# Half a stage of lead for the sample units of a hybrid decoder step, with the new values' block summed last

## The chip, the cores and the metric

The kernel runs on one core of one Trainium2 chip. The metric is the device time of one execution in microseconds; the runs shown are given by their median, and one further execution was profiled.

## The reference, cut to what matters

One inference step of a small decoder trunk: one Conformer convolution layer with its feed-forward, then one attention layer with its feed-forward. It is computed for a prompt of 512 new positions and for 8 sample sequences of 8 new tokens each, all in float32. The attention has 16 heads of 64 and three dilation groups, each with its own queries, keys and values:

```python
WINDOWS = (128, 512, 2048); DILATIONS = (1, 4, 16)
k, v = shared_kv(x, pos, p['kv_norm'], p['w_kv'], p['k_norm'])   # per group, k normed and rotated
q = queries(x, pos, p['b_norm'][j], p['w_q'][j], p['q_norm'][j])
for g in range(N_GROUPS):
    if kv_bufs is None:                                   # prompt: a band of blocks
        o, l = band_attention(q[:, :, g], *keyside[g], r, WINDOWS[g] // r)
    else:                                                 # samples: rows of a cache, then the new ones
        kall = concat([buf[:, :, 0], k_new]); vall = concat([buf[:, :, 1], v_new])
        o, l = gathered_attention(q[:, :, g], *gathered(kall, vall))
x = x + merge_groups(outs, lses, p['w_o'][j], x.dtype)    # softmax over the groups, then w_o
```

The sample part reads keys and values of three caches (128, 512 and 1024 rows per sequence) and appends the 8 new rows of each sequence.

## The kernel before, in words

The convolution (its products lie in a four by four arrangement of 32-wide fields of TensorE, sixteen in all) and the first feed-forward come first; the change does not touch them. Then comes `attention`, which has two parts.

**Projection stages.** `stage(s)` for s = 0 to 3 projects four heads (256 columns) of the queries, keys and values: nine chunks, for kinds 0 (query), 1 (key), 2 (value) and groups 0 to 2. A chunk (`chunk`) takes its matrix of weights from `w_next`, loads a later one on SP's queue (`wraw`), multiplies the prompt's rows in four blocks (`mm3`, L228 to L230, names `pj<-whi,xh`) and the samples' rows once (L1147, `pj<-whi,xs`), and yields five times. Rotated and normed rows are stored to DRAM (`scr` for the prompt, `scs` for the samples' new keys and values) by entries of `due`, at most five ticks later. `new_keys` copies the samples' new queries and keys into `Qz` and `KN`.

**Prompt part.** `prompt()` then runs the band attention of the prompt for 32 pairs of half-blocks, software pipelined: scores (`sc`, L1283), maximum on VectorE, exponential on ScalarE, transposes (`tpt`, L1373), values (`po`, L1395). Its operands come back from DRAM (`nat`, `v`, L1080, L1260, L1264); statistics of the groups go through DRAM in small transfers (`sx`, `ot`, `scc`, `cb`). It yields 88 times.

**Sample units.** The sample attention is cut into eight units, `sample_unit(u)`: unit u handles heads of stage s = u // 2 for four of the eight sequences. A unit is a list of steps, registered by `at(i, order)` under the number `LEAD + u * PERIOD + i`, with PERIOD 32 and LEAD 12, so successive units overlap:

- i = -12 to 31, the keys: nine loads of key blocks (`kk`, 512 KB each, five buffers; L909, L911, L860), their 72 transposes (L920), and the scores (L945) for groups 1, 2 and 0 at i = 14, 26 and 29; the last takes the new keys as well.
- i = 32 to 67, the values: one exponential (`SS`, L966), transposes of the weights (L979), ten loads of value blocks (`vv`, four buffers, each eight steps ahead of its use; L999 to L1010) with ten groups of products summed in `pv` (L1018), scaling, and a small product into `as` (L1031).

Block ti = 1 of the ten holds the new values; it is loaded from `scs` (L1002, three loads of 32 KB), which the value chunks of the same heads have written.

`weave` merges lists of yields by their numbers: the k-th of n goes in at (k + 1) / n. The first 12 sample steps are merged into the end of stage 0, 64 steps into each of stages 1 to 3, and the remaining 100 into the prompt part:

```python
weave((stage(0), 45), (first_loads(), 45))
weave((stage(s), (45, 45, 45)[s - 1]), (islice(samples, WIN[s - 1]), WIN[s - 1]))
weave((prompt(), 2 * NM + 24), (samples, NSAMPLE - LEAD - sum(WIN)))
```

So unit 0's keys run in the first half of stage 1, its values in the second half together with unit 1's keys, and so on; the prompt part runs the values of units 5, 6 and 7 and the keys of units 6 and 7. Every engine executes in the order in which the merged code stands; nearly all DMAs are issued in order on SP's queue. After the prompt part, `merge` splits `ap` and `as` and multiplies with w_o (`pmp<-oh,whi`), and the second feed-forward follows.

Of the kernel before, what the change touches and what calls it, by code (L numbers as in the profile page):

```python
# [90 lines left out]
def trunk(ctx: ExitStack, tc: tile.TileContext, I, O, dbg=None):  # L91
    nc = tc.nc
# [734 lines left out]
    def attention(as_):  # L827
# [26 lines left out]
        def rows2(b, kind, c0):  # L854
            return ck[1][b, :, kind, c0:c0 + CW].rearrange("(j p) c -> p j c", p=128)

        def load3(t, b, kind, c0, q0, q1):
            v = ck[2][b, :, kind, c0:c0 + CW].rearrange("(j q t) c -> t j q c", q=8, t=2)
            for i in range(2):
                nc.sync.dma_start(t[64 * i:64 * i + 64], v[i, :, q0:q1])  # L860

        def kk():
            return sm.tile([128, 4, CW], F32, tag="kk", name="kk", bufs=5)

        KN = {}
        PERIOD, LEAD = 32, 12
        WIN = (64, 64, 64)
        steps = {}

# [16 lines left out]
        pvt = sps.tile([128, CW], F32, name="pv")  # L886

        def sample_unit(u):
# [5 lines left out]
            def at(i, order=1):  # L894
                def put(f):
                    steps.setdefault(LEAD + u * PERIOD + i, []).append((order, f))
                    return f
                return put


            for n in range(9):
                g, bi = (1 + n // 4, n % 4) if n < 8 else (0, 0)
                b = 4 * ub + bi

                @at(3 * n - 12, 2)
                def _(n=n, g=g, b=b):
                    t = Z["k", n] = kk()
                    if g == 0:
                        nc.sync.dma_start(t, ck[0][4 * ub:4 * ub + 4, :, 0, c0:c0 + CW].rearrange("b p c -> p b c"))  # L909
                    elif g == 1:  # L910
                        nc.sync.dma_start(t, rows2(b, 0, c0))  # L911
                    else:
                        load3(t, b, 0, c0, 0, 4)
# [74 lines left out]
                        nc.scalar.activation(ph[:w, a:z], pt[:w, a - tl[0]:z - tl[0]], AF.Copy)  # L988


            for ti in range(10):
                t0 = 41 + 5 * ti // 2

                @at(t0 - 8, 2)
                def _(ti=ti):
                    v = Z["v", ti] = sm.tile([128, 4, CW], F32, tag="vv", name="vv", bufs=4)
                    bs = slice(4 * ub, 4 * ub + 4)
                    if ti == 0:
                        nc.sync.dma_start(v, ck[0][bs, :, 1, c0:c0 + CW].rearrange("b p c -> p b c"))  # L999
                    elif ti == 1:  # L1000
                        for g in range(G):
                            nc.sync.dma_start(v[T * g:T * g + T], scs[2][g][32 * ub:32 * ub + 32, c0:c0 + CW]  # L1002
                                              .rearrange("(b t) c -> t b c", t=T))
                    elif ti < 6:
                        nc.sync.dma_start(v, ck[1][bs, 128 * (ti - 2):128 * (ti - 1), 1, c0:c0 + CW]
                                          .rearrange("b p c -> p b c"))
                    else:
                        vb = ck[2][bs, :, 1, c0:c0 + CW].rearrange("b (j q t) c -> t q j b c", q=8, t=2)
                        for t in range(2):
                            nc.sync.dma_start(v[64 * t:64 * t + 64], vb[t, ti - 6])  # L1010

                @at(t0, 0)
                def _(ti=ti):
                    ph, v = Z["ph"], Z.pop(("v", ti))
                    n = 24 if ti == 1 else 128
                    for bi in range(4):
                        r = slice(32 * bi, 32 * bi + 32)
                        nc.tensor.matmul(pvt[r], ph[:n, ti, r], v[:n, bi], start=ti == 0, stop=ti == 9)  # L1018

            @at(65, 0)  # L1020
            def _():
# [19 lines left out]
        NSAMPLE = max(steps) + 1  # L1041

        def sample_steps():
            for i in range(NSAMPLE):
                for _, f in sorted(steps.get(i, []), key=lambda x: x[0]):
                    f()
                yield


        def weave(*gens):  # L1050

            live = [[g, n, 0] for g, n in gens]
            while live:
                live.sort(key=lambda x: (x[2] + 1) / x[1])
                x = live[0]
                try:
                    next(x[0])
                    x[2] += 1
                except StopIteration:
                    live.remove(x)  # L1060
# [16 lines left out]
        def nat_load(p, g):  # L1077

            t = NAT[p, g] = pnat.tile([128, 8, 128], F32, tag="nat", name="nat", bufs=2)
            nc.sync.dma_start(t, scr[g, :2, :, :, p * 128:p * 128 + 128].rearrange("k r j c -> j (k r) c"))  # L1080

        with xp:
# [116 lines left out]
            def stage(s):  # L1199
                for kind in range(3):  # L1200
                    for g in range(G):
                        yield from chunk(s, kind, g)
# [5 lines left out]
                                  scs[kind][g].rearrange("(b t) c -> b t c", t=T))  # L1208

            samples = sample_steps()  # L1210
            def first_loads():
                yield from range(45 - LEAD)
                yield from islice(samples, LEAD)

            weave((stage(0), 45), (first_loads(), 45))
            for s in range(1, NSTAGE):
                if s == NSTAGE - 1:
                    for g in range(2):
# [7 lines left out]
        with ExitStack() as px:  # L1226
# [12 lines left out]
            def both(m):  # L1239

                return (2 * m, 2 * m + 1)

            def nat_transpose(p, i):
                g, k = divmod(i, 2)
                t = NAT[p, g][:, 4 * k:4 * k + 4]
                pt = ps.tile([128, 512], F32, tag="tpp", name="tpp", bufs=2)
                for r in range(4):
                    x = pt[:, r * 128:(r + 1) * 128]
                    if g == 0:

                        x = pt.rearrange("p (i r jj) -> p r i jj", i=4, r=4)[:, r]
                    nc.tensor.transpose(x, t[:, r], ident)
                d = QK[p, k, g] = pa.tile([128, 512], F32, tag="qk", name="qk", bufs=6)
                nc.scalar.activation(d, pt, AF.Copy)
# [50 lines left out]
            def do_exp(n):  # L1305
                p, lay, e, j = unit(n)
                nb, P = NBS.pop(n), PP[n]
                for ii in range(2):
                    c = cols_of(n, ii)
                    nc.scalar.activation(P[:, ii, c], P[:, ii, c], AF.Exp, scale=SC, bias=nb[:, ii:ii + 1],  # L1310
                                         accum_out=ST[p][:, lay, 2 * j + ii, e, 1:2])
# [92 lines left out]
            NM = NU // 2  # L1404

            def prompt():
                for i in range(5):
                    yield
                for i in range(2):
                    nat_transpose(0, i)  # L1410
                nat_load(0, 2)
                yield
                for m in range(NM + 9):
                    p, k = divmod(m, 4)
                    if 0 <= m - 1 < NM:
                        for n in both(m - 1):
                            do_max(n)
                    if 0 <= m - 3 < NM:
                        do_values(m - 3)
                    yield  # L1420
                    if 0 <= m - 2 < NM:
                        for n in both(m - 2):
                            do_transpose(n)
                    if m < NM:
                        do_scores(m)
                    if 0 <= m - 1 < NM:
                        for n in both(m - 1):
                            do_exp(n)

                    q = p + k // 2  # L1430
                    if k < 3 and q < NP:
                        for i in (2 * k + 2, 2 * k + 3) if k < 2 else (0, 1):
                            nat_transpose(q, i)
                    if k < 3 and p + 1 < NP:
                        nat_load(p + 1, k)
                    if p < NP:
                        if k == 0:
                            v_load(p, 0)
                        elif k == 2:
                            v_load(p, 1)  # L1440
                            v_load(p, 2)
                        elif k == 3 and 1 <= p < 4:
                            new_rows(1, p - 1)
                            new_rows(2, p - 1)
                    for d, f in ((5, exchange), (6, exchanged), (8, coefficients), (9, coefficients_out), (10, coefficients_in),
                                 (12, combine)):
                        if (m - d) % 4 == 0 and 0 <= (m - d) // 4 < NP:
                            f((m - d) // 4)
                    yield

            weave((prompt(), 2 * NM + 24), (samples, NSAMPLE - LEAD - sum(WIN)))
        cx.close()
        return ap

# [97 lines left out]
```

## Time and profile before

| what | us |
|---|---|
| median of 3 runs (2085.93 to 2087.42) | 2086.12 |
| profiled execution | 2083.47 |
| span of its trace, first to last instruction | 2081.5 |
| TensorE (PE) busy in the span | 1972.3 (95%) |
| VectorE / ScalarE / GpSimd busy | 974.0 / 813.0 / 159.8 |
| mean clock granted to TensorE | 0.981 of full |

Times in the trace count from the first instruction. A row of a table by stage gives the stage, its length, the busy time of PE, of PE's weight loads, VectorE, ScalarE and GpSimd with the number of instructions, the granted TensorE clock, the mean busy share of the 16 DMA engines, and the GB/s moved. Rows of waits give the engine and line that waited, the releaser, total us, times, and the longest. In a timeline a bracket at the end is the idle time before the instruction and what ended it.

### The profile page before, as it was taken

The numbers are of one execution on the slowest core, as the hardware profiler recorded it, in microseconds if no ns is written. First come the engines' busy times: TensorE is split into PE (matmuls) and PEld (weight loads), VectorE is DVE, ScalarE is ACT, GpSimd is POOL, SyncE is SP. The second block draws the span as 40 slices with busy tenths as digits, with TensorE's granted clock in tenths as the row PEclk, the third lists the DMA queues.
The fourth block names the chain that finished last, engine by engine and source line by source line (L and its number), as shares of the span: only waits on it lengthen the run. The fifth ranks groups of instructions, "written<-read, shape, count | busy, mean of one in ns | idle before, by whom it ended". The sixth has DMA issues, their size and how long they took to land.

```text
span 2081.5 us, 41730 instructions
## 1 busy us (share of the span) xinstructions
PE 1972.3 (95%) x17621; PEld 1808.7 (87%) x17621; DVE 974.0 (47%) x1868; ACT 813.0 (39%) x1840; POOL 159.8 (8%) x292
## 2 busy tenths in 40 slices
PE   6989799999999999999999999989797999999999
PEld 6657499999999999998889889866565999999998
DVE  5333485432443478465356356325354554324432
ACT  6434554221222344344344344347563332212222
POOL 1000000000000024032022012000012000000000
PEclk9999999999999999999999999989988999999999
DMA  7322066657655855768778877889978665543222
GB/s 209 110 94 102 23 225 226 206 212 277 202 202 183 302 187 161 236 178 237 226 218 223 253 212 212 259 185 227 211 174 209 225 221 195 203 128 82 75 71 74
DMA packets 368877, 387.88 MB, mean 186 GB/s; under 512 B 17983, under 2 KB 357975, under 8 KB 367010
## 3 DMA queue, kind: packets, MB, share of 16 engines
q1 hardware_dynamic: 368130, 384.06, 61.5%
q8 instruction: 139, 2.28, 0.5%
q0 software_dynamic: 560, 1.14, 0.2%
q14 instruction: 48, 0.39, 0.1%
HBM read 348.07 MB, written 146.86 MB: 238 GB/s over the span
## 4 chain that ended last, share of the span: by engine, by line
PE 86%; DMA 6%; ACT 3%; DVE 2%; SPq 2%; issue 1%; another core or an unknown queue 0%; ACTq 0%; DVEq 0%
PE pmm L230 13%; PE pmm L229 13%; PE pmm L228 13%; PE pj L228 7%; PE pj L229 6%; PE pj L230 6%; PE acc L556 3%; PE pj L1147 3%; PE tp L920 3%; PE pmp L229 2%; PE pmp L230 2%; PE pmp L228 2%; PE inp L228 2%; PE tp L945 2%; PE pv L1018 1%; PE inp L229 1%
## 5 line engine op out<-in xcount | busy, mean ns | idle before, releaser
L230 PE MATMUL pmm<-uh,wlo 128*128 128x288 f32 x1344 | 396.2, 295 | 0.0
L228 PE MATMUL pmm<-uh,whi 128*128 128x288 f32 x1344 | 395.9, 295 | 0.0
L229 PE MATMUL pmm<-ul,whi 128*128 128x288 f32 x1344 | 395.7, 294 | 0.0
L228 PE MATMUL pj<-whi,xh 128*128 128x256 f32 x1152 | 331.5, 288 | 0.9 <-DVE xT L766 0.9
L229 PE MATMUL pj<-wlo,xh 128*128 128x256 f32 x1152 | 322.0, 279 | 0.0
L230 PE MATMUL pj<-whi,xl 128*128 128x256 f32 x1152 | 321.7, 279 | 0.0
L229 PEld LDWEIGHTS pmm<-ul,whi 128*128 128x128 f32 x1344 | 252.1, 188 | 0.1
L228 PEld LDWEIGHTS pmm<-uh,whi 128*128 128x128 f32 x1344 | 252.1, 188 | 0.1
L230 PEld LDWEIGHTS pmm<-uh,wlo 128*128 128x128 f32 x1344 | 252.1, 188 | 0.0
L228 PEld LDWEIGHTS pj<-whi,xh 128*128 128x128 f32 x1152 | 216.4, 188 | 10.3 <-issue 9.5
L140 ACT ACTIVATE whi<-wraw 128x1024 fp32r<-128x1024 f32 (+3 forms) x206 | 169.2, 871 | 123.8 <-PE pmm L229 100.6
L229 PEld LDWEIGHTS pj<-wlo,xh 128*128 128x128 f32 x1152 | 216.4, 188 | 0.0
L230 PEld LDWEIGHTS pj<-whi,xl 128*128 128x128 f32 x1152 | 215.9, 187 | 0.0
L141 DVE TENSOR_TENSOR wlo<-wraw,whi 128x1024 fp32r<-128x1024 f32 (+3 forms) x206 | 197.8, 1003 | 24.3 <-ACT whi L140 24.1
L228 PE MATMUL pmm<-hh,whi 128*128 128x288 f32 x704 | 207.6, 295 | 0.0
L230 PE MATMUL pmm<-hh,wlo 128*128 128x288 f32 x704 | 207.5, 295 | 0.0
L229 PE MATMUL pmm<-hl,whi 128*128 128x288 f32 x704 | 207.2, 294 | 0.0
L755 DVE TENSOR_TENSOR gt<-pmm,rs 128x576 f32<-128x576 f32 x42 | 31.8, 758 | 224.5 <-PE pmm L230 224.5
L271 ACT ACTIVATE hh<-gt 128x576 fp32r<-128x576 f32 x44 | 30.2, 687 | 263.3 <-DVE gt L756 263.3
L229 PEld LDWEIGHTS pmm<-hl,whi 128*128 128x128 f32 x704 | 132.1, 188 | 0.0
L228 PEld LDWEIGHTS pmm<-hh,whi 128*128 128x128 f32 x704 | 132.1, 188 | 0.0
L230 PEld LDWEIGHTS pmm<-hh,wlo 128*128 128x128 f32 x704 | 132.0, 188 | 0.0
(292 smaller groups left out, 3510.0 us busy)
## 6 DMA issues: line engine op xcount, KB each, us to landing
out_dram<-in_cache_kv_w_dram SPq DMA_DIRECT2D x64, 1016.0 KB
wraw<-in_w_gate_up_dram SPq DMA_DIRECT2D x88, 512.0 KB
out_dram<-in_cache_kv_w_dram SPq DMA_DIRECT2D x32, 1008.0 KB
wraw<-in_w_kv_dram SPq DMA_DIRECT2D x24, 1024.0 KB
wraw<-in_w_down_dram SPq DMA_DIRECT2D x32, 704.0 KB
kk<-in_cache_kv_w_dram SPq DMA_DIRECT2D x40, 512.0 KB
vv<-in_cache_kv_w_dram SPq DMA_DIRECT2D x40, 512.0 KB
scr<-r SPq DMA_DIRECT2D x36, 512.0 KB
```

Of the source, the lines that this page charges most:

```text
L140: nc.scalar.activation(hi[:, c], raw[:, c], AF.Copy)
L141: wstate["lo"].tensor_sub(lo[:, c], raw[:, c], hi[:, c].bitcast(F32))
L228: nc.tensor.matmul(out, wh, xh, start=start, stop=False)
L229: nc.tensor.matmul(out, wh, xl, start=False, stop=False)
L230: nc.tensor.matmul(out, wl, xh, start=False, stop=stop)
L271: nc.scalar.activation(hi, x, AF.Copy)
L556: nc.tensor.matmul(acc[r][32 * (j - m):32 * (j - m) + 32], DG[c][g, j], exf[c][g, j:S + j], start=m == 0, stop=j + 4 >= TAPS)
L755: nc.vector.tensor_mul(halves(t2), pu, halves(rs))
L920: nc.tensor.transpose(pt[:, j * 128:(j + 1) * 128], Z["k", n][:, j, i * 128:(i + 1) * 128], ident)
L945: nc.tensor.matmul(pt[32 * bi:32 * bi + 32, a:a + n], q[:, x, i, b], kn[:, x, i, T * b:T * b + T] if k is None else k[:, i, bi], start=i = ...
L1018: nc.tensor.matmul(pvt[r], ph[:n, ti, r], v[:n, bi], start=ti == 0, stop=ti == 9)
L1147: nc.tensor.matmul(pt[:, :CW], xs[:, k], x[:, k], start=k == 0 and x is wh, stop=k == KT - 1 and x is wl)
```

## The change

A second number, EARLY = 44, replaces LEAD in the merging (not in the numbering of the steps). 44 sample steps instead of 12 are merged into stage 0, in its last 44 of 64 slots; stages 1 to 3 keep 64 each; the prompt part gets the remaining 68 instead of 100. Every unit thus runs 32 steps, half a stage, earlier. Unit 2s now runs in the second half of the stage that projects its own heads, and its value block ti = 1 would be loaded before the new values are stored; so that block is moved from second to last among the ten, in load and product, and the start and stop of the sum follow the new order.

```diff
-        PERIOD, LEAD = 32, 12
+        PERIOD, LEAD, EARLY = 32, 12, 44
...
-            for ti in range(10):
-                t0 = 41 + 5 * ti // 2
+            for i, ti in enumerate((0, 2, 3, 4, 5, 6, 7, 8, 9, 1)):
+                t0 = 41 + 5 * i // 2
...
-                def _(ti=ti):
+                def _(ti=ti, i=i):
                     ph, v = Z["ph"], Z.pop(("v", ti))
                     n = 24 if ti == 1 else 128
                     for bi in range(4):
                         r = slice(32 * bi, 32 * bi + 32)
-                        nc.tensor.matmul(pvt[r], ph[:n, ti, r], v[:n, bi], start=ti == 0, stop=ti == 9)
+                        nc.tensor.matmul(pvt[r], ph[:n, ti, r], v[:n, bi], start=i == 0, stop=i == 9)
...
-            def first_loads():
-                yield from range(45 - LEAD)
-                yield from islice(samples, LEAD)
-
-            weave((stage(0), 45), (first_loads(), 45))
+            def first_steps():
+                yield from range(64 - EARLY)
+                yield from islice(samples, EARLY)
+
+            weave((stage(0), 45), (first_steps(), 64))
...
-            weave((prompt(), 2 * NM + 24), (samples, NSAMPLE - LEAD - sum(WIN)))
+            weave((prompt(), 2 * NM + 24), (samples, NSAMPLE - EARLY - sum(WIN)))
```

What this moves, at three places. (Lines of the new kernel are one higher from L867 on.)

First, SP's queue in the second half of stage 0, from the store of the new keys of group 0 to that of the second value chunk (`scs_3445` to `scs_3448`: the samples' new rows by kind and group). Before:

```order
L1184 DMA scs_3445<-r_7965 64x256
L1185 DMA scr<-r_7965 128x4x256
L1189 DMA out_dram<-r_7965 128x1x256
L122 DMA wraw<-in_w_kv_dram 128x8x256
L1184 DMA scs_3446<-r_8146 64x256
L1185 DMA scr<-r_8146 128x4x256
L1189 DMA out_dram<-r_8146 512x1x256
```

and now:

```order
L1185 DMA scs_3445<-r_7967 64x256
L1186 DMA scr<-r_7967 128x4x256
L1190 DMA out_dram<-r_7967 128x1x256
L860 DMA kk<-in_cache_kv_w_dram 64x4x256 x2
L122 DMA wraw<-in_w_kv_dram 128x8x256
L860 DMA kk<-in_cache_kv_w_dram 64x4x256 x4
L1185 DMA scs_3446<-r_8152 64x256
L1186 DMA scr<-r_8152 128x4x256
L1190 DMA out_dram<-r_8152 512x1x256
```

The key loads of unit 0, 512 KB in each pair, now stand between the stores and in front of a load of weights.

Second, PE in the first half of stage 1, at the end of the second chunk's prompt rows (`pj` the projections, `kk` a key block, `SS` the weights of the samples' softmax). Before:

```order
L229 MATMUL pj<-wlo,xh 128x256
L230 MATMUL pj<-whi,xl 128x256
L920 MATMUL tp<-ident,kk 128x128 x4
L1147 MATMUL pj<-whi,xs 128x256
L1147 MATMUL pj<-wlo,xs 128x256
```

and now:

```order
L229 MATMUL pj<-wlo,xh 128x256
L230 MATMUL pj<-whi,xl 128x256
L980 MATMUL tp<-ident,SS 128x128
L980 MATMUL tp<-ident,SS 24x128
L921 MATMUL tp<-ident,kk 128x128 x4
L1148 MATMUL pj<-whi,xs 128x256
L1148 MATMUL pj<-wlo,xs 128x256
```

The key transposes that stood there belonged to unit 0 and now belong to unit 1; the value part of unit 0 has joined them.

Third, PE at the end of the prompt part, from the second last group of the prompt's transposes to the end of the last unit (`pv` a value block of a sample unit, `po` the prompt's values, `tpc` the coefficients of a head pair). Before:

```order
L1373 MATMUL tpt<-ident,P 128x128 x8
L1395 MATMUL po<-pts,v 64x128 x8
L1018 MATMUL pv<-vv,ph 32x256 x4
L1373 MATMUL tpt<-ident,P 128x128 x8
L1345 MATMUL tpc<-ident,cf 16x128
L1395 MATMUL po<-pts,v 64x128 x8
L1018 MATMUL pv<-vv,ph 32x256 x12
L1345 MATMUL tpc<-ident,cf 16x128
L1018 MATMUL pv<-vv,ph 32x256 x8
L1031 MATMUL tp<-mf,osb 128x32 x2
```

and now:

```order
L1374 MATMUL tpt<-ident,P 128x128 x8
L1396 MATMUL po<-pts,v 64x128 x8
L1019 MATMUL pv<-vv,ph 32x256 x4
L1374 MATMUL tpt<-ident,P 128x128 x8
L1346 MATMUL tpc<-ident,cf 16x128
L1396 MATMUL po<-pts,v 64x128 x8
L1019 MATMUL pv<-vv,ph 32x256 x8
L1346 MATMUL tpc<-ident,cf 16x128
L1019 MATMUL pv<-vv,ph 32x256 x4
L1032 MATMUL tp<-mf,osb 128x32 x2
```

Behind the prompt's last values stood five value blocks of the last unit, and now three.

## The prediction

> **What bounds the kernel now.** The page comes first: PE is busy nearly all of the span, so work that only changes its place on PE gains nothing.
>
> ```profile
> span 2081.5 us, 41730 instructions
> PE 1972.3 (95%) x17621; PEld 1808.7 (87%) x17621; DVE 974.0 (47%) x1868; ACT 813.0 (39%) x1840; POOL 159.8 (8%) x292
> ```
>
> The attention has to be cut by stage. The timeline gives its first product and the first of the merge behind it; the chain of waits gives the last products of each stage (start, length, x16).
>
> ```profile
> 739.94 0.36 PE L228 MATMUL pj<-whi,xh 128*128 128x256 f32 x1 [0.94 <-DVE xT L766]
> ...
> 860.97 1.89 PE pj L1147 x16
> ...
> 1018.72 2.09 PE pj L1147 x16
> ...
> 1189.31 2.09 PE pj L1147 x16
> ...
> 1359.91 2.10 PE pj L1147 x16
> ...
> 1597.64 0.61 PE L228 MATMUL pmp<-oh,whi 128*128 128x288 f32 x1 [1.04 <-ACT oh L271]
> ```
>
> The table by stage follows: stages 0 to 3, then the prompt part; after the length PE, weight loads, DVE, ACT, POOL, the clock, the DMA share and GB/s.
>
> ```profile
> 739.94:862.86 122.92, 122.92 (x1032) 121.68 (x1033) 86.51 (x181) 50.55 (x127) 34.12 (x64) 1.00 0.60 188
> 862.86:1020.81 157.95, 155.36 (x1448) 142.75 (x1447) 86.87 (x188) 70.13 (x165) 29.39 (x60) 1.00 0.72 208
> 1020.81:1191.40 170.59, 164.51 (x1546) 146.72 (x1545) 87.81 (x191) 72.98 (x173) 29.40 (x60) 1.00 0.81 231
> 1191.40:1362.01 170.61, 164.53 (x1547) 146.74 (x1545) 86.91 (x185) 71.71 (x167) 29.31 (x58) 1.00 0.76 215
> 1362.01:1597.64 235.63, 193.57 (x1926) 139.57 (x1924) 100.05 (x441) 143.00 (x430) 26.37 (x21) 0.90 0.92 199
> ```
>
> Stage 0 is PE without a gap, with the DMA engines at 0.60. The prompt part is the other way round: the DMA engines at 0.92, PE idle for 42.1 us and its clock at 0.90. Its transfers, and PE's three largest waits in it:
>
> ```profile
> DMA packets 67077, 46.81 MB, mean 199 GB/s; under 512 B 8389, under 2 KB 65701, under 8 KB 67051
> ...
> vv<-in_cache_kv_w_dram SPq DMA_DIRECT2D x15, 512.0 KB
> vv<-in_cache_kv_w_dram SPq DMA_DIRECT2D x24, 256.0 KB
> kk<-in_cache_kv_w_dram SPq DMA_DIRECT2D x16, 256.0 KB
> ...
> kk<-in_cache_kv_w_dram SPq DMA_DIRECT2D x6, 512.0 KB
> ...
> vv<-scs SPq DMA_DIRECT2D x9, 32.0 KB
> ```
>
> ```profile
> PE po L1395 <- DMA v<-scr: 8.8, 5, 4.8
> PE tpp L1252 <- DMA nat<-scr: 8.0, 3, 3.8
> PE pv L1018 <- DMA vv<-in_cache_kv_w_dram: 7.1, 4, 2.5
> ```
>
> So the part that the steps leave is paced mostly by transfers, the one they enter by PE. That difference is the whole argument.
>
> **The change part by part.** *Projection stages.* Stages 1 to 3 keep 64 steps each, and units differ only in heads and sequences. Stage 1 becomes what stage 2 is, 170.6 instead of 157.95, since the values of unit 0 join the keys of unit 1: +12.6. Stages 2 and 3 stay. Stage 0 gets the keys of one unit without values. A full stage holds two units and costs (170.59 - 122.92) / 2 = 23.8 us for each; less the 12.6 of the values the keys cost 11.2. Together **+23.8 us**. No row shows keys in stage 0 itself. The upper bound takes the keys at their full PE time in the first half of stage 1, 11.24 for the transposes and 4.92 for the scores, 16.2 instead of 11.2, so 28.8:
>
> ```profile
> 862.85:940.00 77.15, 11.24 (x80) 8.86 (x78) 1.00 0.62 181
> ...
> 862.85:940.00 77.15, 4.92 (x96) 1.82 (x96) 1.00 0.62 181
> ```
>
> The lower bound is 20: from stage 0's standing start some of the 6.1 us that stage 2 leaves PE idle may not come. I take 23.8, from whole stages. The queue that the key loads pass is SP's: they stand ahead of weights and stores. In stage 2 the same neighbours stand there at a DMA share of 0.81, and PE's idle time is 6.1 us in all, already inside the 23.8; stage 0 has more room (0.60). ScalarE's copies of the keys likewise: 73 of 170.6 us busy in stage 2, 50 of 122.9 in stage 0. If that cover were gone, a chunk late by a whole transfer of weights would show as PE waiting for `whi`.
>
> *Prompt part.* It loses the keys of one unit of two and the values of one of three. PE's groups there (count | busy, mean ns | idle before):
>
> ```profile
> L920 PE MATMUL tp<-ident,kk 128*128 128x128 f32 x144 | 23.7, 294 | 1.5 <-ACT kt L929 0.9 <-ACT ph L988 0.4
> L1018 PE MATMUL pv<-vv,ph 128*32 128x256 f32 (+1 forms) x240 | 21.4, 431 | 7.1 <-DMA vv<-in_cache_kv_w_dram 7.1
> L945 PE MATMUL tp<-kt,Qz 128*32 128x512 f32 x64 | 8.8, 672 | 0.0
> L979 PE MATMUL tp<-ident,SS 128*128 128x128 f32 (+1 forms) x30 | 5.8, 315 | 0.7 <-ACT kt L929 0.6
> L1031 PE MATMUL tp<-mf,osb 128*128 128x32 f32 x16 | 3.2, 333 | 3.1 <-ACT kt L929 2.5 <-DVE osb L1024 0.6
> ```
>
> PE loses (23.7 + 8.8) / 2 + (21.4 + 5.8) / 3 + 3.2 / 4 = 26.1 us, from 193.6 to 167.5. The DMA engines lose 18 blocks of 512 KB and three of 32 KB, 9.5 of 46.8 MB. By bytes at the same mean rate the part would take 235.6 x 37.3 / 46.8 = 188 us. By packets (rows of 1 KB, so 9312 of 67077) it would take 203 us. Neither price is shown alone in the trace; I take the middle, **195 us, a change of -40.6**, which leaves PE 27 us of idle time. A rule bears on the choice between bytes and packets: the Trainium skill, DMA: Bandwidth & Descriptors, section Why small descriptors are slow (HBM only), gives a packet its 32-byte beats plus about three. An estimate by that page takes 326 thousand of 1664 thousand beats away, a part of 189 us and a sum 6 us lower; no row here separates the two.
>
> *The end of the prompt part.* The chain of waits there, behind the prompt's last values in PE's timeline:
>
> ```profile
> 1575.01 1.09 PE L1395 MATMUL po<-pts,v 128*64 128x128 f32 x14 [0.17 <-DVE pts L1376]
> ...
> 1569.02 11.36 DMA vv<-in_cache_kv_w_dram
> ...
> 1580.40 5.70 DMA sx<-st
> ...
> 1588.46 5.26 DMA vv<-in_cache_kv_w_dram
> ```
>
> 21.5 us pass from these values to the merge, under loads of the last unit's value blocks. With 68 steps over 88 yields instead of 100, the big ones are issued before that. This gain, between 0 and 11.4 + 5.3 = 16.7 us, is a part of the 40.6 and not added.
>
> *The moved block.* The same products and loads change places: 0. Its loads now stand right ahead of the last `sx` exchange on SP's queue; at worst it costs one such transfer, 5.7 us, at best it saves the wait for stored rows earlier in the unit, under 1 us. The work of the units behind it hides it except in the last one.
>
> *Sum.* +23.8 - 40.6 = -16.8. From the profiled execution of 2083.5 this gives 2066.7; that execution was 2.6 under the median, so the median goes to 2069.3.
>
> **The rivals.** *The clock comes back too (faster still).* PE's clock falls after idle stretches:
>
> ```profile
> 1427.66 0.88 PE L1395 MATMUL po<-pts,v 128*64 128x128 f32 x12 [0.52 <-DMA v<-scr]
> ...
> 1479.72 0.69 PE L1395 MATMUL po<-pts,v 128*64 128x128 f32 x4 [4.76 <-DMA v<-scr]
> 1481.49 1.55 PE L1395 MATMUL po<-pts,v 128*64 128x128 f32 x12 [1.07 <-DMA v<-scr]
> ...
> 1400.00:1440.00 40.00, 37.88 (x450) 27.58 (x445) 20.23 (x96) 28.46 (x91) 0.00 (x0) 1.00 1.04 221
> ...
> 1480.00:1520.00 40.00, 35.40 (x308) 24.14 (x306) 19.10 (x83) 23.35 (x69) 7.54 (x6) 0.84 1.03 235
> ```
>
> Twelve products take 0.88 us, and 1.55 after a wait of 4.76; the stretches run at 1.00 and 0.84. If the long waits go, PE needs 167.5 x 0.90 = 151 us, and with 25 idle the part takes 176: 23.8 - 59.6 = -36, **2050**. Against it: DMA busy at 1.03 in these stretches, which must fall first. The Trainium skill, TensorE: Matmul & The Clock Gate, section HAM oscillation — how this bites in real kernels, puts the clock's fall at idle gaps over about 3.4 us; by that rule it is the wait of 4.76 that must shrink, and the trace agrees as far as these rows go.
>
> *Only PE's own time moves (no change).* If the waits stay in length, the part takes 235.6 - 26.1 = 209.5: 23.8 - 26.1 = -2.3, **2084**. For it: in 1400 to 1440 PE is busy for 37.9 of 40. Against it: 24 us of waits on DMA elsewhere.
>
> *The prompt's own loop sets the pace (slower).* Scores, maximum, exponential, transposes and values of one half-block follow each other over three engines; sample work may only fill their gaps. Then the idle time grows as PE's work goes, only the end shrinks, by the 16.7, and 23.8 - 16.7 = +7.1, **2093**. It decides if the part shrinks by less than 23.8. Against it: ACT is busy for 143.0 and DVE for 100.1 of 235.6 us, and one of the transfers in that loop's statistics, 8 KB, is long for a reason that more bandwidth cures:
>
> ```profile
> 1419.64 8.23 DMA ot<-sx
> ```
>
> **How the numbers follow.** 0.2%, or 4.2 us, is about what a measurement here can tell from no change. Forecast (part at 187 to 203, 2061 to 2077): 0.62. Clock: 0.12. No change: 0.15. Slower: 0.11. Faster is 0.74, the same 0.15, slower 0.11. The range leaves out the slower rival and the lower half of the clock's, and takes in the other bounds: 2055 to 2086.
>
> **What would show it.** Stage 0 should take 134 us and stage 1 170.6, with stages 2 and 3 as they were; PE in the prompt part should be busy for about 167 us with some 37 MB moved in about 195; less than 15 us should pass from the prompt's last values to the merge. The forecast is wrong if PE waits for `whi` in stage 0, if the prompt part still takes over 205 us, or if its idle time does not fall under 35 us.

## The result, and the profile after

The changed kernel takes 2069.1 us in the median (2063.7 to 2072.2, 5 runs) against 2086.1 (2080.5 to 2088.7, 5 runs): a ratio of 0.9918, 95% interval 0.9895 to 0.994. In a second comparison, with an experiment further on, the ratio was 0.9913 (0.9892 to 0.9934). The forecast was 2069.3.

The profiled execution took 2069.12 us. Its page, first lines:

```profile
span 2067.3 us, 41746 instructions
PE 1968.2 (95%) x17621; PEld 1807.9 (87%) x17621; DVE 975.2 (47%) x1868; ACT 813.0 (39%) x1840; POOL 158.6 (8%) x292
```

The table by stage of the changed kernel, cut at the same instructions as before: stages 0 to 3, then the prompt part.

```profile
736.88:873.72 136.84, 136.10 (x1200) 131.44 (x1201) 87.07 (x189) 60.24 (x145) 32.18 (x64) 1.00 0.66 199
873.72:1042.00 168.28, 163.80 (x1542) 146.13 (x1541) 87.41 (x190) 72.88 (x172) 29.39 (x60) 1.00 0.87 228
1042.00:1212.48 170.48, 164.40 (x1547) 146.61 (x1545) 87.81 (x191) 72.98 (x173) 29.39 (x60) 1.00 0.83 230
1212.48:1382.96 170.48, 164.40 (x1546) 146.61 (x1545) 86.89 (x185) 71.70 (x167) 29.30 (x58) 1.00 0.80 215
1382.96:1581.11 198.15, 167.31 (x1665) 124.82 (x1663) 101.37 (x431) 130.57 (x406) 23.91 (x20) 0.92 0.83 186
```

The stages last 646.1 us instead of 622.1 (+24.0), the prompt part 198.15 instead of 235.63 (-37.5). In the prompt part PE is busy 26.3 us less and idle for 30.8 instead of 42.1; the DMA share falls from 0.92 to 0.83. What lies ahead of stage 0 was 3.1 us shorter in this profile, and what follows the prompt part 2.3 longer: +24.0 - 37.5 - 3.1 + 2.3 = -14.3, from a span of 2081.5 to 2067.3 but for rounding. The 3.1 is no effect of the change: stage 0 began between 733.7 and 742.1 us in the profiles of this study. The second comparison's profile of the changed kernel gives +25.3 for the stages and -32.9 for the prompt part:

```profile
1382.90:1585.65 202.75, 169.72 (x1666) 125.46 (x1663) 99.37 (x431) 130.28 (x406) 24.32 (x20) 0.89 0.78 182
```

The prompt part's transfers, and PE's largest waits in it:

```profile
DMA packets 57238, 36.93 MB, mean 187 GB/s; under 512 B 7936, under 2 KB 55936, under 8 KB 57216
...
vv<-in_cache_kv_w_dram SPq DMA_DIRECT2D x10, 512.0 KB
...
vv<-in_cache_kv_w_dram SPq DMA_DIRECT2D x16, 256.0 KB
...
kk<-in_cache_kv_w_dram SPq DMA_DIRECT2D x8, 256.0 KB
```

```profile
PE sc L1284 <- DVE st L1296: 7.6, 6, 2.8
PE tpp L1253 <- DMA nat<-scr: 5.2, 1, 5.2
PE po L1396 <- DMA v<-scr: 4.0, 3, 1.7
PE tpc L1346 <- DVE cf L1342: 3.6, 2, 2.1
```

The wait for the last unit's value blocks (7.1 us before) is gone, those for the prompt's own operands fell from 16.8 to 9.2, and waits of the scores for VectorE have taken first place: the prompt's own loop shows.

The end of the part in PE's timeline: of the kernel before the prompt's last values, behind the group at 1575.01 that the prediction shows, and of the changed kernel from the last values to the merge.

```profile
1578.21 1.37 PE L1395 MATMUL po<-pts,v 128*64 128x128 f32 x16
```

```profile
1573.35 1.09 PE L1396 MATMUL po<-pts,v 128*64 128x128 f32 x16
1574.37 1.07 PE L1019 MATMUL pv<-vv,ph 128*32 128x256 f32 x16
1577.59 0.27 PE L1346 MATMUL tpc<-ident,cf 128*16 128x128 f32 x1 [2.14 <-DVE cf L1342]
1577.79 0.63 PE L1019 MATMUL pv<-vv,ph 24*32 24x256 f32 x8
1579.03 1.06 PE L1032 MATMUL tp<-mf,osb 128*128 128x32 f32 x4 [0.61 <-DVE osb L1025]
1581.11 0.61 PE L228 MATMUL pmp<-oh,whi 128*128 128x288 f32 x1 [1.02 <-ACT oh L271]
1582.89 0.61 PE L229 MATMUL pmp<-ol,whi 128*128 128x288 f32 x1 [1.18 <-DVE ol L272]
```

From the last values to the merge it was 1597.64 - 1579.58 = 18.1 us and is now 1581.11 - 1574.44 = 6.7. So 11.4 of the 37.5 us come from the end. The table by stage for the stretch ahead of the end, before and after:

```profile
1362.00:1579.60 217.60, 187.69 (x1881) 137.55 (x1879) 97.64 (x430) 141.62 (x425) 20.40 (x17) 0.92 0.94 204
```

```profile
1383.00:1574.40 191.40, 164.33 (x1639) 123.22 (x1638) 98.96 (x420) 129.18 (x400) 22.59 (x18) 0.92 0.85 190
```

Of its 26.2 us PE's busy time makes up 23.4; its idle time went only from 29.9 to 27.1 us. The merge then starts a little worse: its second product waits 1.18 us more.

### The profile page after: what moved, and what is told of

It is laid out like the page before. It is cut to its first block, busy times and chain, and to the rows that moved or that the text cites. A ratio compares the mean times of both kernels' runs of the same rounds, so it can differ in the third digit from the quotient of the medians.

```text
span 2067.3 us, 41746 instructions
## 1 busy us (share of the span) xinstructions
PE 1968.2 (95%) x17621; PEld 1807.9 (87%) x17621; DVE 975.2 (47%) x1868; ACT 813.0 (39%) x1840; POOL 158.6 (8%) x292
## 4 chain that ended last, share of the span: by engine, by line
PE 88%; DMA 4%; ACT 3%; DVE 3%; SPq 1%; issue 1%; another core or an unknown queue 0%; ACTq 0%; DVEq 0%
PE pmm L230 13%; PE pmm L229 13%; PE pmm L228 13%; PE pj L228 7%; PE pj L229 7%; PE pj L230 7%; PE acc L556 3%; PE pj L1148 3%; PE tp L921 3%; PE pmp L229 2%; PE pmp L230 2%; PE pmp L228 2%; PE tp L946 2%; PE pv L1019 2%; PE inp L228 2%; PE inp L229 1%
## 5 line engine op out<-in xcount | busy, mean ns | idle before, releaser
L228 PEld LDWEIGHTS pj<-whi,xh 128*128 128x128 f32 x1152 | 216.4, 188 | 11.4 <-issue 10.8
L141 DVE TENSOR_TENSOR wlo<-wraw,whi 128x1024 fp32r<-128x1024 f32 (+3 forms) x206 | 197.7, 1003 | 24.1 <-ACT whi L140 23.9
```

The lines of the kernel that those rows point to most:

```text
L141: wstate["lo"].tensor_sub(lo[:, c], raw[:, c], hi[:, c].bitcast(F32))
L228: nc.tensor.matmul(out, wh, xh, start=start, stop=False)
```

## The experiments

Each length of the prompt part below is of one profile and carries several us of spread, which the runs of the changed kernel show (198.2 and 202.7); the 235.6 of the kernel before is of an execution 2.6 us under its median. So the medians count first. Ratios are to the kernel before on the same chip, with 95% intervals.

**Only the order of the value blocks.** The second half of the diff without the lead:

```diff
-            for ti in range(10):
-                t0 = 41 + 5 * ti // 2
+            for i, ti in enumerate((0, 2, 3, 4, 5, 6, 7, 8, 9, 1)):
+                t0 = 41 + 5 * i // 2
...
-                        nc.tensor.matmul(pvt[r], ph[:n, ti, r], v[:n, bi], start=ti == 0, stop=ti == 9)
+                        nc.tensor.matmul(pvt[r], ph[:n, ti, r], v[:n, bi], start=i == 0, stop=i == 9)
```

> The kernel before with the new values' block moved last, the units at their old places. By the forecast (the move costs nothing): stages 0 to 3 at 122.9, 158, 170.6 and 170.6 us as before, the prompt part at 235.6 within 3, total within 0.2% of before. Rival (the late loads of new values stand in front of the last exchange on SP's queue): the last unit ends up to 5.7 us later.

Ratio 1.0017 (0.9997 to 1.0036): 2089.9 against 2087.0 us. The row of the prompt part:

```profile
1357.24:1605.79 248.55, 195.93 (x1929) 141.25 (x1927) 99.76 (x441) 142.94 (x431) 26.40 (x21) 0.88 0.87 188
```

The stages kept their lengths. The prompt part was 13 us longer in this profile, of an execution of 2092 us (at most 3 were expected), but its end was not: 15.2 us from the last values to the merge against 18.1. The exchange behind the late loads is therefore not what made it longer, and the interval reaches from no effect to +7.5 us. The move is no gain; whether it costs a few us at the old places stays open.

**A quarter of the last unit's loads.** Its transposes and products all read the one part that is loaded.

```diff
+            nl = 1 if u == 7 else 4
...
-                        nc.sync.dma_start(t, rows2(b, 0, c0))
+                        nc.sync.dma_start(t[:, :nl], rows2(b, 0, c0)[:, :nl])
...
-                        ... Z["k", n][:, j, i * 128:(i + 1) * 128]
+                        ... Z["k", n][:, j % nl, i * 128:(i + 1) * 128]
...
-                            nc.sync.dma_start(v[64 * t:64 * t + 64], vb[t, ti - 6])
+                            nc.sync.dma_start(v[64 * t:64 * t + 64, :nl], vb[t, ti - 6])
```

> The kernel before; the last unit loads only one of four parts of each of its 18 cache blocks (its results are from that part), 7.1 MB and 6912 packets less in the prompt part, PE's work and the number of DMAs unchanged. Theory T (transfers pace the prompt part): it shortens by about three quarters of the 37.5 us that the change took from it, some 20 to 28, to 208 to 216 us. Theory F (PE's own work went, transfers are hidden): by less than 5, over 230 us.

Ratio 0.9919 (0.9892 to 0.9946), 18.9 us. The prompt part:

```profile
1363.91:1588.58 224.67, 190.01 (x1928) 138.49 (x1926) 102.11 (x441) 143.08 (x430) 26.43 (x21) 0.93 0.78 176
```

With every instruction of PE still there, taking bytes away shortens the kernel: the theory that transfers pace the part holds against the one that only PE's work counts. In the profile it is 11 us, under the 20 expected, and 8 of them at the end (10.1 us from the last values to the merge); but the profiled execution, 2075.1 us, was the slowest of four, and by the medians the gain lies just under the 20.

**Half runs for the keys of the last two units.** Runs of 512 B instead of 1 KB:

```diff
+            nw = CW // 2 if u >= 6 else CW
...
-                        nc.sync.dma_start(t, rows2(b, 0, c0))
+                        nc.sync.dma_start(t[:, :, :nw], rows2(b, 0, c0)[:, :, :nw])
```

> The kernel before; the last two units load only the first 128 of 256 columns of each key block (both halves are computed from these), so 18 blocks come in runs of 512 B instead of 1 KB: 4.7 MB less in the prompt part, the same number of packets, PE's work unchanged. Theory T by bytes: the prompt part shortens by about 4.7 / 46.8 of its length or more, 18 to 24 us. Theory T by packets: by less than 4. Theory F: by less than 3.

Ratio 0.9926 (0.9903 to 0.995), 16.8 us. Its transfers and its prompt part:

```profile
DMA packets 67139, 43.35 MB, mean 195 GB/s; under 512 B 8398, under 2 KB 65710, under 8 KB 67113
...
1360.61:1583.14 222.53, 189.56 (x1929) 137.24 (x1927) 103.73 (x441) 142.69 (x431) 26.43 (x21) 0.93 0.86 195
```

The packets are as many as before (67128 in the whole prompt part there, with 47.0 MB), the bytes fewer by some 3.7 MB (the rest of the 4.7 lay ahead of the part), and the time falls by 13 us in the profile and 17 in the median. By packets it would not have fallen, by bytes by 18: the price is nearly that of the bytes. The records of single packets say the same, and those of the kernel before said it already: in its prompt part a packet of 512 B took 37 ns in the mean and one of 1 KB 76. The Trainium skill, DMA: Bandwidth & Descriptors, section Why small descriptors are slow (HBM only), adds only about three beats to a packet; an estimate by that rule is 19 beats for 512 B and 35 for 1 KB, nearly the same per byte, and the trace agrees (37 and 76 ns).

**A quarter of the last unit's work on PE,** its loads whole:

```diff
+            nl = 1 if u == 7 else 4
...
-                        for j in range(4):
+                        for j in range(nl):
                             nc.tensor.transpose(pt[:, j * 128:(j + 1) * 128], ...
...
-                    for bi in range(4):
+                    for bi in range(nl):
                         r = slice(32 * bi, 32 * bi + 32)
```

> The kernel before; the last unit transposes one of four parts of each key block (ScalarE copies it four times) and multiplies one of four sequences in its value blocks; all its loads stay. PE loses three quarters of 11.9 and of 7.1 us, some 14 us, in the prompt part. Theory T: it shortens by less than 5. Theory F: by about 14. If both count alike: 5 to 10.

Ratio 0.9989 (0.9973 to 1.0006), 2083.0 against 2087.0 us: not clear of no change. The prompt part:

```profile
1355.63:1596.54 240.91, 191.89 (x1814) 136.51 (x1812) 101.04 (x441) 143.28 (x430) 26.36 (x21) 0.87 0.88 194
```

PE is busy only 1.9 us less, and the reason lies first in the edit. It takes out 54 transposes and 60 products, but not the 14 us of the expectation. The rows of the two groups in this run, for the 23.7 and 21.4 us that the prediction shows:

```profile
L921 PE MATMUL tp<-ident,kk 128*128 128x128 f32 x90 | 18.0, 309 | 2.1 <-ACT kt L934 1.3 <-ACT ph L992 0.6
L1022 PE MATMUL pv<-vv,ph 128*32 128x256 f32 (+1 forms) x180 | 21.5, 439 | 4.6 <-DMA vv<-in_cache_kv_w_dram 4.6
```

The transposes give 5.7 us and the products nothing: those of the four sequences of a block lie in four 32-wide fields and ran beside each other. The products of one block of the last unit, in the kernel before and in this run:

```profile
1572.06 0.64 PE L1018 MATMUL pv<-vv,ph 128*32 128x256 f32 x8
```

```profile
1572.98 0.62 PE L1022 MATMUL pv<-vv,ph 128*32 128x256 f32 x2
```

So the run takes some 6 us of PE's work away and not 14, and says little of what PE's work is worth. The other groups took nearly 4 us longer at a clock of 0.87 instead of 0.90, and the idle time is 49 us instead of 42; the run with the order alone, which has all of PE's work, shows the like (0.88, and 53 us idle), so this is within the spread of single executions.

**Both cuts together** (the two edits in one kernel):

> The kernel before; the last unit loads one of four parts of its cache blocks and does only a quarter of its key transposes and value products (the edits of the two runs that did each alone together): 7.1 MB and some 14 us of PE less in the prompt part. Alone they took 11 us (loads) off the prompt part and nothing (PE). Theory C (two limits, transfers first and PE right behind): together more than the sum, 18 to 28 us off, to 208 to 218. Rival S (only transfers count): the same as the loads alone, 222 to 228.

Ratio 0.9915 (0.9881 to 0.9949), 16.7 us.

```profile
1356.72:1578.78 222.06, 183.29 (x1815) 132.22 (x1813) 101.53 (x441) 142.66 (x431) 26.44 (x21) 0.93 0.80 178
```

This is the loads alone again (0.9919); the theory that PE stands right behind the transfers in the last unit did not hold, as far as a cut of some 6 us of PE's work can tell (its transposes fell from 23.7 to 17.7 us, its products from 20.1 to 19.9).

**The same cuts a third of the part earlier,** for the value blocks of unit 5 and the keys of unit 6 (`nv = 1 if u == 5 else 4`, `nl = 1 if u == 6 else 4`), the loads first:

> The kernel before; a quarter of the loads for the value blocks of unit 5 and the key blocks of unit 6, the first third of the prompt part where the DMA engines are busy at 1.03 (in the run with the last unit's loads cut, those lay in the later two thirds). Again 7.1 MB less, some key loads of it ahead of the prompt part; PE's work unchanged. Theory P (a transfer is worth its time only where the DMA engines are saturated): the prompt part shortens by 20 to 30 us, total ratio 0.986 to 0.990. Rival (the place does not matter): by 11 to 17, ratio 0.992.

Ratio 0.9935 (0.9914 to 0.9956), 12.5 us, and 6 us of the prompt part in the profile: not the 20 to 30 that saturated engines would give. It took 5.5 MB out of the part; the rest lay ahead of it. Then with PE's cuts as well:

> The same with PE's key transposes of unit 6 and value products of unit 5 cut to a quarter as well, 14 us of PE. Theory P alone: as the loads alone, within 4 us. Rival (once the transfers go, PE is next): 6 to 12 us more than the loads alone, which would be near the whole 37 to 41 us that the change took off the prompt part.

Ratio 0.9913 (0.9883 to 0.9943), 19.1 us. The prompt parts of the two:

```profile
1358.26:1587.62 229.36, 191.32 (x1929) 136.74 (x1927) 100.28 (x441) 142.65 (x431) 26.38 (x21) 0.90 0.82 181
...
1356.57:1580.29 223.72, 185.43 (x1814) 131.60 (x1812) 101.99 (x441) 142.23 (x430) 26.44 (x21) 0.91 0.81 185
```

Here PE's cut brings some 6 us on top (5.6 in the profiles, 6.6 in the medians), and PE's busy time falls by 5.9 and not by the 14 expected (its transposes from 23.9 to 17.0, its products from 22.7 to 21.2). The intervals of the ratios overlap, so this is likely rather than shown; and the two together stay at 19 us, far from the 37 to 41 of the whole unit.

**Half the move:** `EARLY = 28`.

> The changed kernel with a lead of 28 steps instead of 44, half the move: 84 steps stay in the prompt part. Stages 0 and 1 together +12 instead of +24. Theory linear: prompt part -19, total -7, about 2080. Theory transfers first (the first bytes taken away are worth most): prompt part -24 or more, total -12, about 2075.

Ratio 0.9974 (0.9948 to 1.0001): not clear of no change. Its stages 0 to 3 last 130.2, 166.2, 176.3 and 171.6 us, 22 more than before in place of 12. Why is not shown: a unit's keys and values now meet the chunks at other points, and the granted clock was 0.99 and 0.97 in stages 1 and 2 of this profile, where it was 1.00 in the kernel before. The prompt part:

```profile
1378.58:1584.10 205.52, 173.04 (x1830) 125.95 (x1828) 98.78 (x437) 134.35 (x413) 25.38 (x21) 0.95 0.88 198
```

30 us are gone from it with 16 of the 32 steps, as the theory that the first bytes are worth most had it (in an execution of 2071.1 us, among the fastest of this kernel); the price in the stages, which no theory had, ate the gain.

**More than the move:** `EARLY = 52`, then 54 beside the changed kernel unaltered.

> The changed kernel with a lead of 52 steps, 8 more out of the prompt part. Projection stages +6 over the changed kernel. If transfers still pace the prompt part: another 9 us off it, total 3 under the changed kernel, ratio to before about 0.990. If PE and the other engines now set its pace: 5 to 6 off, no gain over the changed kernel, ratio 0.992.

> The changed kernel with a lead of 54 steps, the most that the new keys allow. From the lead of 52 (projection stages 655, prompt part 184, ratio 0.9891): projection stages +1 to +3, prompt part -1 to -4, ratio 0.987 to 0.990 and 4 to 8 us under the changed kernel. If the 52 was a lucky profile and the gain ends at 44: ratio 0.991 to 0.993.

> The changed kernel unaltered, for a comparison with the next on one chip: ratio to before 0.9918 within its interval of 0.9895 to 0.994; prompt part 194 to 204 us, projection stages 646.

The lead of 52: ratio 0.9891 (0.9864 to 0.9917); stages 655.6 us, prompt part 183.7. The lead of 54: 0.9884 (0.9865 to 0.9903), 2063.2 us (2059.6 to 2065.3), against 0.9913 and 2068.6 (2063.0 to 2072.9) for the changed kernel on the same chip; stages 647.2, prompt part 191.6. The prompt parts of the two leads:

```profile
1393.19:1576.84 183.65, 155.37 (x1635) 113.92 (x1633) 98.19 (x429) 125.39 (x396) 23.75 (x19) 0.97 0.79 184
...
1381.28:1572.84 191.56, 162.53 (x1618) 118.92 (x1616) 99.85 (x429) 124.80 (x393) 23.18 (x19) 0.93 0.76 171
```

Both are faster than before. The lead of 52 cost the stages 9.5 us over the first profile of the changed kernel and took 14.5 off the prompt part, where 6 and 9 were expected. Over the changed kernel the lead of 54 is some 5 us faster in the medians, with intervals that overlap. The totals came out as expected and the split did not: from the lead of 52 to that of 54 the stages were to cost 1 to 3 us more, and were 8 shorter, while the prompt part was 8 longer, at a clock of 0.93 instead of 0.97. In this one profile the stages of the lead of 54 cost no more than those of a lead of 44 (646.1 and 647.4), though ten more steps lie in them: stage 0 takes 4.5 us more, and stages 1 and 2 take 168.1 us each instead of 168.2 and 171.9 in the run beside it (168.3 and 170.5 in the first).

**A denser end:** the last 68 steps merged as if there were 78.

> The changed kernel with its last 68 sample steps merged as if there were 78, so that the last unit ends before the prompt does. If the last unit's value blocks still set the end: the stretch from the prompt's last values to the merge shortens by 2 to 5 us. If the prompt's own exchange of statistics sets it: by less than 2, and denser transfers ahead may cost 0 to 5; ratio to before 0.990 to 0.994.

Ratio 0.9919 (0.9885 to 0.9952), no change to the changed kernel. The end shrank from 6.7 to 4.2 us, as expected if the last unit's value blocks still set it; the part as a whole was 201.5, within the 198.2 and 202.7 of the changed kernel, so no gain from it is shown.

## Why the prediction was right, and where its steps were off

*The sum* was forecast at 2069.3 and measured 2069.1, and that it is so close is in part luck. The terms of the first profile come to +24.0 - 37.5 + 2.3 = -11.2, those of the second to +25.3 - 32.9 + 1.6 = -6.0, where -16.8 was forecast. The rest lies in what the change does not touch: the stretch ahead of stage 0 (3.1 and 4.4 us shorter) and the profiled executions, of which that of the kernel before was 2.6 us under its median and the second of the changed kernel 4.2 over. An estimate from the medians, -17.0 less 24.0 and 2.3, puts the prompt part's change at some -43. The forecast of -40.6 lies between that and the profiles; they fix it to no better than some 10 us.

*The projection stages* were forecast at +23.8 and measured +24.0 and +25.3 in the two profiles. Whole stages were the right yardstick for the sum. The split was off, with two misses that cancel, for which the step gave no reason: stage 0 took 13.9 more instead of 11.2, stage 1 10.3 instead of 12.6. PE waits 0.7 us in stage 0 for a copy and never for weights, so the loads in front of them on SP's queue were covered.

*PE's work and the bytes in the prompt part* were forecast at 167.5 us and 37.3 MB and measured 167.3 and 36.9 (169.7 us in the second profile).

*The prompt part* was forecast at 195 us, between 188 by bytes and 203 by packets, and measured 198.2 and 202.7. The step chose a middle between two prices because it found neither in the trace; the packets' own times (37 and 76 ns) were there, and they and the half runs show that bytes are nearly the right one of the two. By bytes alone the part would have come down to 188 or, by the estimate from the Trainium skill, to 189. In the profiles the time went with PE instead: its busy time fell by 26.3 of the 37.5 us, and ahead of the end by 23.4 of 26.2, while PE's idle time there fell by only 2.8.

*The reason*, a part paced mostly by transfers, is thus half right. Three quarters of a unit's transfers alone gave 12 to 19 us with all of PE's instructions in place, so transfers do set part of the pace. Some 6 us of PE's work gave 4 us or nothing alone, and the two together 17 to 19, where the whole unit gave 17 net of the 24 in the stages, that is about 41. What the cuts left in place was a quarter of the loads, some 20 of PE's 26 us, all copies on ScalarE, all DMA issues on SP's queue, and the unit's place at the end. The runs do not tell these apart, and how the rest of the 41 divides stays open. One rival was not tested. SP's queue, which issues the loads in order, itself waits for PE: the load of the prompt's next operand (`nat`, two buffers) for the transposes of an earlier one. Ahead of the end, before and after:

```profile
SPq L1080 <- PE tpp L1252: 23.8, 7, 6.1
```

```profile
SPq L1081 <- PE tpp L1253: 22.5, 12, 3.6
```

If loads wait for PE and PE for loads, two separate limits are the wrong picture: less work on either would bring the other forward. This is argued and not shown; a run with more buffers for `nat` would tell.

*The end* was expected under 15 us and is 6.7. The step read the wrong row: the products at 1575.01 were not the prompt's last, those at 1578.21 were, so the stretch before was 18.1 and not 21.5. The gain of 11.4 lies inside the 0 to 16.7 that the step gave.

*The moved block* was put at 0. At the old places it cost between nothing and 7.5 us; at the new ones no run tests it alone.

*The rivals.* The clock stayed at 0.92 and 0.89 in the two profiles, so it did not come back (with a lead of 52 it was 0.97). That only PE's own time moves (2084) was ruled out for the whole by the median, by the end and by the run with fewer loads; for the stretch ahead of the end it is nearly what the profile shows. The prompt's own loop did not set the pace (2093), but its scores' waits on VectorE have grown from 4.4 to 7.6 us.

*Not in the sum:* the 2.3 us behind the prompt part (1.6 in the second profile). The merge's first 22 us run at a clock of 0.82 instead of 0.90, and its second product waits for VectorE:

```profile
1597.64:1620.00 22.36, 22.24 (x151) 21.92 (x152) 17.21 (x25) 11.37 (x23) 4.43 (x3) 0.90 0.94 342
```

```profile
1581.11:1603.50 22.39, 21.21 (x135) 20.89 (x136) 14.24 (x23) 10.36 (x23) 7.67 (x5) 0.82 0.94 333
```

## What to carry to other kernels

Work that is moved out of a stage with two high loads, here 92% of the DMA engines and 82% of PE, is not priced by a cut of one resource: three quarters of a unit's loads gave 12 to 19 us, where the whole unit gave about 41. And an edit that takes out instructions has to be checked for the busy time it takes out: 114 instructions fewer were 6 us of PE and not 14. Price the stage that the work enters by whole stages that already hold such work: here this came within 2 us in sum, though not for each stage. When background steps are merged with a foreground by their numbers, do not expect the price to follow their number: in one profile each, half the move cost the stages nearly as much as all of it, and ten steps more cost them nothing.

## What the runs showed of the hardware that had not been expected

Products that lie in different 32-wide fields took no time beside each other: eight of them, for four sequences, took 0.64 us and two, for one sequence, 0.62, so that three quarters of them could go without PE being busy any less. And runs of 512 B cost hardly more per byte than runs of 1 KB: a packet took 37 against 76 ns in the mean, and the same number of packets with 3.7 MB less moved in 13 us less.
